# A hybrid attention and convolution block on Trainium2: two more taps of the second convolution block in the second pair, three more in the third, none in the fourth, and the branch's norm started among the fourth pair's projections

## The chip, the core and the metric

The kernel runs on one core of one Trainium2 chip. The metric is the device time of one execution in microseconds (us), lower is better. All times of instructions come from one profiled execution of the kernel before. PE is TensorE's matmul queue, PEld its weight loads, DVE is VectorE, ACT is ScalarE, POOL is GpSimd, SP is SyncE, which issues most of the DMAs.

## The reference

The input is 1024 latent positions and 256 context positions of 1024 channels, all in float32. They are normalised and modulated, and one projection gives eleven column groups to three branches. Their outputs, side by side, go through one output projection, a gated residual and a final norm. The change lies in the third branch (`conformer_branch`) and in the time that the second branch (`neighbourhood_attention`) leaves for it.

```python
def layernorm(x, g, b):
    xf = x.astype(jnp.float32)
    mu = jnp.mean(xf, axis=-1, keepdims=True)
    var = jnp.mean(jnp.square(xf - mu), axis=-1, keepdims=True)
    y = (xf - mu) * lax.rsqrt(var + LN_EPS)
    return (y * g.astype(jnp.float32) + b.astype(jnp.float32)).astype(x.dtype)

def short_conv_branch(z_h, z_b, z_c, z_g, w_conv):
    return z_b * dwconv(z_c * z_h, w_conv) * jax.nn.silu(z_g)

def conformer_branch(z_p, z_q, z_g, w_conv, b_conv, ln_g, ln_b):
    u = z_p * jax.nn.sigmoid(z_q)
    u = dwconv(u, w_conv) + b_conv.astype(u.dtype)
    u = layernorm(u, ln_g, ln_b)
    return jax.nn.silu(u) * jax.nn.silu(z_g)
...
    hl = rmsnorm(x, norm_g[l]) * (1.0 + scale[:, None, :]) + shift[:, None, :]
    hc = rmsnorm(ctx, norm_g[l]) * (1.0 + scale_c) + shift_c
    zl = jnp.split(hl @ w_in[l], PROJ_SPLITS, axis=-1)
...
    ya = short_conv_branch(zl[0], zl[1], zl[2], zl[3], conv_sc[l])
    yb = neighbourhood_attention(heads(zl[4]), heads(zl[5]), heads(zl[6]), kc, vc, rpb[l])
    yb = yb * jax.nn.silu(zl[7])
    yc = conformer_branch(zl[8], zl[9], zl[10], conv_cf[l], conv_cf_b[l], ln_cf_g[l], ln_cf_b[l])
    y = jnp.concatenate([ya, yb, yc], axis=-1) @ w_out[l]
```

The convolution of the third branch has 31 taps over positions, for 256 channels, which are two blocks of 128. Its layer norm runs over the 256 channels of one position, so it needs all taps of both blocks. Attention has 8 heads of 64 channels; each query sees a window of the grid with a bias, and all context keys.

## The kernel before

**Matmuls.** Channels lie on partitions, positions along the free axis. Every matrix product is made of three matmuls on split operands (high weight by high input, high by low, low by high): lines L329, L330 and L331 for one step of 128 input channels by 512 positions. Eight such steps fill one bank (`ps_z`) of which there are three; then a *sink* empties it. The weights of one projection come in two loads (L310, tile `wr`), and each is split: the high part on ACT (L129, `wh`), the low part on POOL (L130, `wl`), or on DVE where the weights of k are scaled on the way (L322).

**The stages.** After the start and the projections of the first two heads come the values of all heads, and then four heads' pairs, one after the other; the code numbers them 0 to 3, and the text says first to fourth. A pair first makes q and k (`proj_pair`): two banks for q (sink L357 on ACT and L358 on DVE), two for k and half a bank for the context keys (sink L379 on ACT and L380 on DVE, each once for each of the pair's two heads). Then `attend` runs 16 blocks of attention, each one head by 128 queries, with 48 steps of projection work (the *fill*: the pair's gate first, then what the other two branches need) strewn between them, so that PE has work while the softmax runs elsewhere. The last pair's fill is its gate, half of the second short convolution's input, and its middle part (`sc_mid`). After the pairs come what is left of the fill, the third branch's gate, and the output projection.

**A block of attention.** Scores go to the one score tile `ps_s` (L596 window keys, L597 context keys). DVE adds the bias and finds the minimum (L601, which has a second row for the readout of `mn`), ACT takes the exponential with its sum (L604), DVE the reciprocal (L605), POOL scales (L606, tile `pr`). Two blocks later PE transposes (L615, `ps_t`), ACT and DVE write the high and low part (L619, L620, `pw`), and one block later PE multiplies by the values (L627, `po`). After two blocks `fold` adds the parts of `po` into `yb` (L572 on ACT, L576 and L578 on DVE). The queries of four blocks are copied by two DMAs (L364) ahead of the blocks that read them.

**The third branch.** Its taps are DVE instructions over 128 channels by 1024 positions, one for each tap (L692 for all but the first of a block), which add into one tile (`acc`). The first block's 31 run while the values are made. The second block's 31 are dealt out to the second, third and fourth pair by `conv_part`: 13, 13 and 5. When all are done `cf_norm` runs in eight steps, two halves of four. A step of the first kind transposes 256 positions to put channels on the free axis (four L713), takes statistics (L718, L719 on DVE), a reciprocal root on POOL (L269, L271), and normalises (two L724 on DVE). Two of these are followed by two steps of the second kind, which transpose back (four L734), apply tanh on ACT (L736) and two DVE passes (L739, L741) into `acc`. Each step uses a bank of `ps_z`, from the same three that the projections use, and each half of the norm uses four of the tiles `t`.

**What sets the order.** On PE the order is that of the code: `run` takes projection steps one after the other, and each PE group adds its estimated length to a clock (`self.pe`). A piece given to `spawn` is put in between: its next part comes when that clock has passed its due time, which is the delay given, and then the gap that the piece yields (1.6 between taps, 3.0 between steps of the norm). On the other engines a list scheduler orders the instructions; each tap is only tied to come after the matmul that stood before it in the code. Every engine runs its own list strictly in order.

Of the kernel before, what the change touches and what calls it, by code (L numbers as in the profile page):

```python
# [65 lines left out]
class Builder:  # L66
# [985 lines left out]
    def build(self):  # L1052
# [68 lines left out]
        for pair in range(1, 4):  # L1121
            self.pair_alloc()
            self.v_alloc()
            self.v_load(pair)
            self.spawn(self.conv_part((13, 13, 5)[pair - 1], 1.6))
            self.run(self.proj_pair(pair))
            if pair == 3:
                self.spawn(self.cf_norm(), 6.0)
            self.attend(pair, itertools.chain(self.proj_gate(pair), fill), MF[pair])
        self.run(fill)  # L1130
        self.drain()
# [83 lines left out]
```

## Time and profile before

| | us |
|---|---|
| median of 3 runs | 612.09 (611.95 to 612.26) |
| the profiled execution | 610.97 |
| its span (first to last instruction) | 609.2 |
| the second pair's q and k, from | 215.3 |
| its attention, from | 242.6 |
| the third pair's q and k, and attention, from | 301, 329.05 |
| the fourth pair's q and k, and attention, from | 386.6, 414.15 |
| what follows the fourth attention, from | 479.5 |

The granted clock of TensorE was 0.997 of full speed over the span. In the rows of a timeline the first number is the start in us from the start of the span, the second the duration in us; then come engine, line, operation, output and input tiles with partitions by elements, and in brackets how long the engine had been idle and what ended that. An "x4" joins four instructions in a row, and the duration is then that of all. "64x256" and the like are partitions by elements of one instruction. The recorded ends of matmuls are modelled, so a group of matmuls is best measured from its start to the next one's.

### The profile page before, as it was taken

How to read it: one execution, taken by the hardware profiler on the slowest of the kernel's cores; microseconds unless marked ns; L12 is line 12 of the kernel's file. 1: busy time of each engine (PE TensorE's matmuls, PEld its weight loads, DVE VectorE, ACT ScalarE, POOL GpSimd, SP SyncE). 2: the span in 40 equal slices, each digit the busy share in tenths (PEclk: the TensorE clock that was granted, in tenths of full speed). 3: DMA queues.
4: the chain of work that ended last, by engine and by line, in shares of the span. 5: the costliest groups of instructions: out<-in, count | busy, mean ns of one | idle time of the engine just before them, and what ended most of it. 6: DMA issues, size and time to landing. Idle time of an engine off the chain costs nothing.

```text
span 609.2 us, 8937 instructions
## 1 busy us (share of the span) xinstructions
PE 589.7 (97%) x3101; PEld 493.8 (81%) x3101; DVE 400.7 (66%) x681; ACT 245.9 (40%) x470; POOL 182.1 (30%) x194
## 2 busy tenths in 40 slices
PE   7899999999999999999999999999999999999995
PEld 5566888888888888888888888888788888888885
DVE  4466988765676699578897666936889447383222
ACT  2555822111455432544423554425645334124222
POOL 1021233000443222333112332113433370099311
PEclk9999999999999999999999999999999999999998
DMA  8992585976533136332145242172301454951122
GB/s 285 356 335 63 190 272 169 115 156 180 121 86 77 24 91 167 75 81 54 41 138 128 48 113 56 45 215 65 81 19 36 137 166 147 341 177 36 70 103 104
DMA packets 97170, 78.64 MB, mean 129 GB/s; under 512 B 26507, under 2 KB 80869, under 8 KB 96997
## 3 DMA queue, kind: packets, MB, share of 16 engines
q1 hardware_dynamic: 95397, 71.51, 42.4%
q10 hardware_dynamic: 1728, 6.55, 3.0%
q8 instruction: 25, 0.41, 0.3%
q14 instruction: 20, 0.16, 0.1%
HBM read 55.93 MB, written 14.29 MB: 115 GB/s over the span
## 4 chain that ended last, share of the span: by engine, by line
PE 84%; DVE 5%; ACT 3%; issue 2%; DMA 2%; POOL 2%; SPq 1%; POOLq 0%; DVEq 0%; ACTq 0%
PE ps_z L329 14%; PE ps_z L331 14%; PE ps_z L330 14%; PE po L627 5%; PE ps_f L878 5%; PE ps_f L879 5%; PE ps_f L877 5%; PE ps_t L615 4%; PE ps_z L419 3%; PE ps_z L421 3%; PE ps_s L596 3%; PE ps_z L420 3%; PE ps_s L597 2%; DMA wr<-in_w_in 2%; PE ps_h L279 1%
## 5 line engine op out<-in xcount | busy, mean ns | idle before, releaser
L329 PE MATMUL ps_z<-h,wh 128*128 128x512 f32 x384 | 151.1, 394 | 0.0
L331 PE MATMUL ps_z<-h,wl 128*128 128x512 f32 x384 | 150.3, 391 | 0.0
L330 PE MATMUL ps_z<-h,wh 128*128 128x512 f32 x384 | 149.8, 390 | 0.0
L130 POOL TENSOR_TENSOR wl<-wr,wh 128x512 fp32r<-128x512 f32 x44 | 60.8, 1384 | 167.3 <-ACT wh L129 160.3
L606 POOL TENSOR_SCALAR pr<-pr,sm 128x640 f32<-128x640 f32 (+1 forms) x64 | 56.6, 884 | 138.2 <-DVE sm L605 118.1
L331 PEld LDWEIGHTS ps_z<-h,wl 128*128 128x128 f32 x384 | 72.1, 188 | 16.1
L330 PEld LDWEIGHTS ps_z<-h,wh 128*128 128x128 f32 x384 | 72.1, 188 | 12.4
L329 PEld LDWEIGHTS ps_z<-h,wh 128*128 128x128 f32 x384 | 72.1, 188 | 12.1
L692 DVE SCALAR_TENSOR_TENSOR acc<-t,half_w,acc 128x1024 f32<-128x1024 f32 x60 | 81.1, 1351 | 1.2
L619 ACT ACTIVATE pw<-ps_t 128x640 fp32r<-128x640 f32 (+1 forms) x64 | 43.5, 680 | 90.1 <-PE ps_t L615 89.9
L601 DVE CUSTOM_DVE_ANT_0 ps_s<-ps_s,bt 128x640 f32<-128x640 f32 (+1 forms) x64 | 50.9, 796 | 29.4 <-PE ps_s L597 27.1
L620 DVE TENSOR_TENSOR pw<-ps_t,pw 128x640 fp32r<-128x640 f32 (+1 forms) x64 | 50.4, 788 | 16.0 <-ACT pw L619 15.8
L604 ACT ACTIVATE pr<-ps_s,mn 128x640 f32<-128x640 f32 (+1 forms) x64 | 49.0, 766 | 19.4 <-DVE mn L601 18.5
L627 PE MATMUL po<-pw,vt 128*128 128x256 f32 x304 | 51.3, 297 | 4.1 <-DVE yb L578 3.1
L878 PE MATMUL ps_f<-wol,y 128*128 128x512 f32 (+1 forms) x136 | 51.6, 379 | 0.0
L879 PE MATMUL ps_f<-woh,y 128*128 128x512 f32 (+1 forms) x136 | 51.5, 379 | 0.0
L877 PE MATMUL ps_f<-woh,y 128*128 128x512 f32 (+1 forms) x136 | 51.5, 379 | 0.0
L129 ACT ACTIVATE wh<-wr 128x512 fp32r<-128x512 f32 x46 | 29.0, 630 | 42.3 <-PE ps_z L330 21.0
L627 PEld LDWEIGHTS po<-pw,vt 128*128 128x128 f32 x304 | 40.5, 189 | 6.4 <-issue 4.7
L615 PE MATMUL ps_t<-ident,pr 128*128 128x128 f32 x304 | 43.6, 272 | 0.0
L596 PE MATMUL ps_s<-kt,qd 128*128 128x384 f32 (+1 forms) x128 | 39.6, 331 | 0.5 <-ACT pr L604 0.4
L615 PEld LDWEIGHTS ps_t<-ident,pr 128*128 128x128 f32 x304 | 35.6, 141 | 1.4 <-issue 0.4
(177 smaller groups left out, 923.9 us busy)
## 6 DMA issues: line engine op xcount, KB each, us to landing
wr<-in_w_in SPq DMA_DIRECT2D x52, 256.0 KB
wa<-in_w_ada SPq DMA_DIRECT2D x16, 512.0 KB
qd<-qn SPq DMA_DIRECT2D x32, 256.0 KB
vd<-t SPq DMA_DIRECT2D x20, 256.0 KB
x_in<-in_x SPq DMA_DIRECT2D x8, 512.0 KB
t<-in_w_ada SPq DMA_DIRECT2D x16, 256.0 KB
vt<-vd SPq DMA_DIRECT2D x32, 128.0 KB
fraw<-in_w_out SPq DMA_DIRECT2D x8, 512.0 KB
```

The lines of the kernel that those rows point to most:

```text
L130: i2 = (eng or nc.vector).tensor_tensor(out=lo, in0=src, in1=f32(hi), op=ALU.subtract)
L329: nc.tensor.matmul(ps, lhsT=wh, rhs=hh, start=(k == 0), stop=False)
L330: nc.tensor.matmul(ps, lhsT=wh, rhs=hl, start=False, stop=False)
L331: self.last = nc.tensor.matmul(ps, lhsT=wl, rhs=hh, start=False, stop=(k == KT - 1))
L596: nc.tensor.matmul(win, lhsT=q[:, b % 4], rhs=kwin, start=(i == 0), stop=(i == 1))
L606: nc.gpsimd.tensor_scalar(out=pr, in0=pr, scalar1=sm, scalar2=0.5, op0=ALU.mult, op1=ALU.mult)
L615: nc.tensor.transpose(out=pt[:, c * P:(c + 1) * P], in_=pr[:, c * P:(c + 1) * P], identity=self.ident)
L627: self.nc.tensor.matmul(po, lhsT=vt[:, vi, h], rhs=pw[:, c], start=(c == 0), stop=(c == n - 1))
L692: self.after_pe(nc.vector.scalar_tensor_tensor(out=acc, in0=u[:, t:t + T], scalar=self.half_w[:, 2 * t + ct:2 * t + ct + 1], in1=acc, op0= ...
L877: nc.tensor.matmul(ps, lhsT=yh, rhs=wh[:, ch], start=(first and i == 0), stop=False)
L878: nc.tensor.matmul(ps, lhsT=yh, rhs=wl[:, ch], start=False, stop=False)
L879: nc.tensor.matmul(ps, lhsT=yl, rhs=wh[:, ch], start=False, stop=(last and i == len(chs) - 1))
```

## The change

The taps of the second block are dealt out 15, 16 and 0 in place of 13, 13 and 5, and `cf_norm` is spawned ahead of the fourth pair's q and k with a delay of 2.0, in place of after them with 6.0. Its eight steps are unchanged, and so is their gap.

```diff
             self.v_load(pair)
-            self.spawn(self.conv_part((13, 13, 5)[pair - 1], 1.6))
+            self.spawn(self.conv_part((15, 16, 0)[pair - 1], 1.6))
+            if pair == 3:
+                self.spawn(self.cf_norm(), 2.0)
             self.run(self.proj_pair(pair))
-            if pair == 3:
-                self.spawn(self.cf_norm(), 6.0)
             self.attend(pair, itertools.chain(self.proj_gate(pair), fill), MF[pair])
```

How this moves instructions is seen best at three places. The first is DVE in the second pair, from the last two sinks of k to the first block's softmax; `64x8x8x8` is a sink of 512 latent keys, `64x256` one of the context keys. Before:

```order
L692 SCALAR_TENSOR_TENSOR acc<-t_1472,half_w,acc 128x1024
L380 TENSOR_TENSOR kt<-ps_z,kt 64x8x8x8
L380 TENSOR_TENSOR kt<-ps_z,kt 64x256 x2
L601 ISA ps_s,mn<-ps_s,bt_1194 128x512
L601 ISA mn 128x1
L605 RECIPROCAL sm<-sm 128x1
```

And in the changed kernel, at the same place:

```order
L692 SCALAR_TENSOR_TENSOR acc<-t_1472,half_w,acc 128x1024
L380 TENSOR_TENSOR kt<-ps_z,kt 64x8x8x8
L692 SCALAR_TENSOR_TENSOR acc<-t_1472,half_w,acc 128x1024
L380 TENSOR_TENSOR kt<-ps_z,kt 64x256
L692 SCALAR_TENSOR_TENSOR acc<-t_1472,half_w,acc 128x1024
L380 TENSOR_TENSOR kt<-ps_z,kt 64x256
L601 ISA ps_s,mn<-ps_s,bt_1194 128x512
L601 ISA mn 128x1
L605 RECIPROCAL sm<-sm 128x1
```

The two added taps stand ahead of the sinks of the context keys, and so ahead of the first block's L601. The third pair has the same rows, and its third added tap stands behind the first L601 and ahead of the L605.

The second place is DVE at the start of the fourth pair, where the third pair's last blocks end (L620, and the fold, L576 and L578) and the sinks of q begin (L358). Before:

```order
L576 TENSOR_TENSOR yb<-po,fold 64x16x16
L578 TENSOR_TENSOR yb<-po,yb 64x16x16
L692 SCALAR_TENSOR_TENSOR acc<-t_1472,half_w,acc 128x1024 x2
L620 TENSOR_TENSOR pw<-ps_t,pw 128x4x128
L692 SCALAR_TENSOR_TENSOR acc<-t_1472,half_w,acc 128x1024
L358 TENSOR_TENSOR qn<-ps_z,qn 128x8x8x8
```

And in the changed kernel, where `t_4018` and `t_4061` are the normalised tiles of the first two steps:

```order
L576 TENSOR_TENSOR yb<-po,fold 64x16x16
L718 BN_STATS bnst<-ps_z 128x6
L578 TENSOR_TENSOR yb<-po,yb 64x16x16
L719 BN_AGGR bnmv<-bnst 128x2
L718 BN_STATS bnst<-ps_z 128x6
L719 BN_AGGR bnmv<-bnst 128x2
L724 TENSOR_SCALAR t_4018<-ps_z,bnmv,bnrs 128x256 x2
L620 TENSOR_TENSOR pw<-ps_t,pw 128x4x128
L718 BN_STATS bnst<-ps_z 128x6 x2
L719 BN_AGGR bnmv<-bnst 128x2 x2
L724 TENSOR_SCALAR t_4061<-ps_z,bnmv,bnrs 128x256 x2
L358 TENSOR_TENSOR qn<-ps_z,qn 128x8x8x8
```

Taps are gone from this place, and the first two steps of the norm stand around the L620 of the third pair's last block and ahead of the first sink of q. The second half of the norm stands among the sinks of k in the same way.

The third place is SP's list of DMAs at the start of the fourth pair, as one piece of the difference.

```order
 L444 DMA vt<-vd 128x2x256
 L563 DMA yd_63<-yb 128x1024
+L310 DMA wr<-in_w_in 128x4x128 x2
 L364 DMA qd<-qn 64x2x512 x4
-L310 DMA wr<-in_w_in 128x4x128 x4
+L310 DMA wr<-in_w_in 128x4x128 x2
 L509 DMA bt_1198<-u_1053 24x1x64
```

Two of the four weight loads (L310) that stood behind the q loads (L364) stand ahead of them.

## The prediction

> **What bounds the kernel now.** I read the page first: the busy shares, then the chain that ended last. TensorE (PE) is busy for 97% of the span and carries 84% of the chain, so a microsecond counts only where PE stands still for it.
>
> ```profile
> PE 589.7 (97%) x3101; PEld 493.8 (81%) x3101; DVE 400.7 (66%) x681; ACT 245.9 (40%) x470; POOL 182.1 (30%) x194
> PE 84%; DVE 5%; ACT 3%; issue 2%; DMA 2%; POOL 2%; SPq 1%; POOLq 0%; DVEq 0%; ACTq 0%
> ```
>
> Then the table of stretches, for the stages that the change touches: the attention of the second pair, the projections of the fourth, the attention of the fourth, where the norm now runs. The columns are the stretch, its length, and busy us and instructions of PE, weight load, DVE, ACT and POOL.
>
> ```profile
> 240.50:301.00 60.50, 60.30 (x356) 52.95 (x355) 43.23 (x94) 31.58 (x66) 20.83 (x22) 1.00 0.25 61
> 386.60:414.10 27.50, 27.50 (x141) 23.41 (x140) 14.95 (x20) 8.48 (x16) 6.14 (x5) 1.00 0.48 135
> 414.10:480.00 65.90, 62.78 (x381) 54.02 (x381) 52.32 (x124) 33.81 (x67) 22.90 (x30) 1.00 0.20 47
> ```
>
> PE idles 60.50 - 60.30 = 0.2 us in the second pair's attention, nothing in the fourth pair's projections, and 65.90 - 62.78 = 3.1 us in the fourth pair's attention. The second pair fills its attention with the same work as the fourth (a gate, half of a short-convolution input, its middle), but has no norm. So moving the norm aims at about 2.9 us of idle PE, and those projections have DVE time to spare (14.95 of 27.50 us).
>
> **The norm leaves the fourth pair's attention.** What it costs there is idle time (two rows of the table of waits of 414 to 480: sum, count, longest) and starts that come late (the timeline):
>
> ```profile
> PE po L627 <- DVE yb L578: 1.6, 2, 0.9
> PE ps_z L734 <- DVE t L724: 0.9, 2, 0.5
> ...
> 429.91 0.78 PE L734 MATMUL ps_z<-ident,t 128*128 128x128 f32 x2 [0.38 <-DVE t L724]
> 430.46 0.41 PE L596 MATMUL ps_s<-kt,qd 128*128 128x384 f32 x1
> 434.77 0.60 PE L734 MATMUL ps_z<-ident,t 128*128 128x128 f32 x4
> 435.13 0.42 PE L596 MATMUL ps_s<-kt,qd 128*128 128x384 f32 x1
> 463.90 0.83 PE L627 MATMUL po<-pw,vt 128*128 128x256 f32 x5 [0.76 <-DVE yb L578]
> ```
>
> The idle part is 3.1 - 0.2 = 2.9 us. Some waiting is counted as busy: two transposes took 0.55 us to the next start at 429.91, where four that waited for nothing took 0.36 us at 434.77, so some 0.37 us is hidden. I estimate 1.9 us at six such places. Together 4.8 us. The wait of 0.76 us at 463.90 lies behind the short convolution's taps, after the norm's end; I leave it, so **-4.1 us**. Bounds: the norm's own two waits (0.9) and the longer fold wait (0.9) alone, -1.8; everything, -4.8. The 32 transposes themselves, eight groups of about 0.36 us, move and are paid in either place.
>
> **The norm arrives among the projections.** There are now eight more tenants for the three z banks, and the order on DVE puts each norm step in line with the sinks of q and k. One step takes, by its rows here:
>
> ```profile
> 441.72 0.60 PE L713 MATMUL ps_z<-ident,acc 128*128 128x128 f32 x4
> 442.36 0.76 DVE L718 BATCH_NORM_STATS2 bnst<-ps_z 128x6 f32<-128x256 f32 x2 [0.85 <-PE ps_z L713]
> 443.70 0.70 POOL L271 TENSOR_TENSOR bnrs<-bnrs,mhalf 128x2 f32<-128x2 f32 x1
> 444.44 1.00 DVE L724 TENSOR_SCALAR t<-ps_z,bnmv,bnrs 128x256 f32<-128x256 f32 x2 [0.15 <-POOL bnrs L271]
> ...
> 393.10 0.63 PE L627 MATMUL po<-pw,vt 128*128 128x256 f32 x4
> 393.57 0.39 PE L329 MATMUL ps_z<-h,wh 128*128 128x512 f32 x1
> 394.26 0.40 PE L329 MATMUL ps_z<-h,wh 128*128 128x512 f32 x1
> ...
> 410.74 0.63 ACT L129 ACTIVATE wh<-wr 128x512 fp32r<-128x512 f32 x1 [0.70 <-PE ps_z L330]
> 435.46 0.78 ACT L736 ACTIVATE t<-ps_z,half_ln 128x512 f32<-128x512 f32 x1 [0.76 <-PE ps_z L734]
> ```
>
> From the transposes' start to the normalised tile is 445.44 - 441.72 = 3.7 us. Between a second group of L713 and the L734 that reads it, PE has some 3.3 us (four steps of 394.26 - 393.57 = 0.69, a values group of 393.57 - 393.10 = 0.47) in the first half, 3.4 us (five steps) in the second. In the first half, DVE comes to the statistics 0.4 us late, behind L620: PE waits about 0.4 + 3.7 + 0.05 - 0.4 (the transposes' own time) - 3.25, which is 0.5 us. In the second half two L380 sinks of 0.69 us stand in between, of which about 0.7 us is not covered: again 0.5. A third wait follows at the gate: its bank is that of k's second half, and the second L379 of that sink now stands behind a weight split (L129, 0.63 us) that itself waits for PE, 0.4 us. Sum **+1.4 us**. Bounds: 0 if PE's lead holds everywhere, and 2.7 if one split on POOL (L130, 1.29 us) also gets ahead of a reciprocal root. Behind a waiting L724 stand the L620 of the third pair's last block and the L358 of q; PE needs neither before its next wait. On SP two weight loads now precede the four q loads; these are issued some 4 us later, and still land well before the scores. ACT's four tanh of 0.78 us have ACT's 19 idle us. The five taps that leave these projections delayed no PE instruction (its idle there is 0), so they give nothing.
>
> **Two taps more in the second pair, three in the third.** DVE does not run them in a gap: the order puts tap 14 ahead of the first L380 of the context keys, and tap 15 ahead of the second, which stands ahead of the first block's bias pass, L601. The rows at that place, second pair:
>
> ```profile
> 239.36 1.29 DVE L692 SCALAR_TENSOR_TENSOR acc<-t,half_w,acc 128x1024 f32<-128x1024 f32 x1
> 240.02 3.04 POOL L130 TENSOR_TENSOR wl<-wr,wh 128x512 fp32r<-128x512 f32 x2 [11.12 <-ACT wh L129]
> 240.68 0.69 DVE L380 TENSOR_TENSOR kt<-ps_z,kt 64x512 fp32r<-64x512 f32 x1
> 241.66 0.42 DVE L380 TENSOR_TENSOR kt<-ps_z,kt 64x256 fp32r<-64x256 f32 x1 [0.30 <-ACT kt L379]
> 242.53 0.43 DVE L380 TENSOR_TENSOR kt<-ps_z,kt 64x256 fp32r<-64x256 f32 x1 [0.45 <-ACT kt L379]
> 242.71 0.28 PE L597 MATMUL ps_s<-kt,qd 128*128 128x256 f32 x1
> 243.26 0.70 DVE L601 CUSTOM_DVE_ANT_0 ps_s<-ps_s,bt 128x512 f32<-128x512 f32 x1 [0.31 <-PE ps_s L597]
> 244.11 0.69 ACT L604 ACTIVATE pr<-ps_s,mn 128x512 f32<-128x512 f32 x1 [1.62 <-DVE mn L601]
> 244.70 0.19 ACT L604 ACTIVATION_READ_ACCUMULATOR pr<-ps_s,mn 128x1 f32 x1
> 245.15 0.34 PE L596 MATMUL ps_s<-kt,qd 128*128 128x384 f32 x1
> ```
>
> There is one score tile (ps_s): the second block's scores at 245.15 need the first block's exponential, which ends at 244.70 + 0.19 = 244.89. With the 0.05 to 0.15 us of a hand-over the slack is 0.1 us. So what L601 loses beyond 0.1 us PE loses, and nothing later gives it back: PE's own work between scores is fixed, and the next block's chain is as tight.
>
> How late is L601? Unhindered: tap 14 from 241.40, L380 at 242.71, tap 15 at 243.15, L380 at 244.46, L601 at 244.92: 1.66 us late, 1.55 us lost. But POOL splits weights at that moment, and taps and splits do not run at once:
>
> ```profile
> 224.77 1.29 POOL L130 TENSOR_TENSOR wl<-wr,wh 128x512 fp32r<-128x512 f32 x1 [9.25 <-ACT wh L129]
> 224.85 2.29 DVE L692 SCALAR_TENSOR_TENSOR acc<-t,half_w,acc 128x1024 f32<-128x1024 f32 x1
> ```
>
> A tap issued 0.08 us behind a split took 2.29 us in place of 1.28. At 240.02 it was the other way round: the first split sat through tap 13 (to 240.65), and the pair ended at 243.06, 1.2 us each. So tap 14 meets the first split: it starts at 241.7 and ends at 242.95; the second split takes 242.95 to 244.1, L380 runs beside it, tap 15 starts at 243.9 and ends at 245.2, the last L380 ends at 245.65, and L601 starts at 245.7: 2.44 late, **2.3 us lost**. If both splits run ahead of tap 14, it is 246.4 and 3.0 us. The third pair's rows repeat this place to within 0.1 us, its splits included; its third tap (16) stands behind L601, where ACT's 0.9 us of exponential hide most of it, and if that cover is gone a reciprocal comes 0.4 us later into 2.6 us of slack before the transposes that need it. So twice 2.3, **+4.6 us**; bounds 3.1 and 6.0.
>
> [...]
>
> **Sum.** -4.1 + 1.4 + 4.6 = +1.9 us. The profiled execution took 610.97 us (span 609.2), so 612.9 by its own clock. The median of the runs, 612.09, is 1.1 us above it; added there, **614.0 us**.
>
> **Rivals.**
> 1. *No collision.* DVE gets in before each split, taps cost 1.55 each: +3.1 + 1.4 - 4.1 = +0.4, 612.5 us. For it: at 240.02 POOL waited. Against: tap 14 comes due while the first split runs.
> 2. *Faster: the score chain absorbs the taps.* If PE waits only for the first context keys (L597 at 243.2 in place of 242.7, 0.5 us), and the second block's scores do not follow L601, then 1.0 + 1.4 - 4.1 = -1.7, 610.4 us. It decides at the second L596 of each attention: it needs 1.5 us of slack there. Against it stand 244.89 and 245.15.
> 3. *Much slower.* Splits run ahead of both taps (6.0), and a root waits for a split on POOL (2.7), against the same gain: +4.6, 616.7 us.
> 4. *The change doesn't do what it says.* The order shows both moves, so this is left only as part of the cases above: the fold waits may stay without the norm (gain 1.8), for +4.2, 616.3 us.
>
> **How the numbers follow.** The forecast has 0.48 (its own range 613 to 615.5), rival 1 0.22, rival 2 0.13, rivals 3 and 4 together 0.17. A measurement of this kernel tells about 0.2%, 1.2 us, from no change. Faster by more: rival 2, 0.13. Within: rival 1 and a tenth of the forecast, 0.27. Slower: the rest, 0.60. The range runs from rival 2 to a little beyond rival 3: 610.2 to 617.0.
>
> **What would show it.** Right: PE waits of 0.5 to 1 us before the first L597 of the second and third attention and over 1 us before the second L596; taps of over 2 us beside L130 there; idle PE under 1.2 us in the fourth attention; waits for L724 in the fourth projections, 1.4 us with the gate's. Wrong: second scores on time in spite of late L601, or a fourth attention that keeps its 3 us of idle PE.

## The result, and the profile after

The changed kernel takes 615.58 us (median of 4 runs, 615.51 to 616.27), the kernel before 612.06 (4 runs, 611.95 to 612.26). The ratio is 1.006, with a 95% interval of 1.0042 to 1.0077: slower by 3.5 us, where 1.9 was forecast. The time lies just above the forecast's own range, 613 to 615.5 us, and within the range over all cases, 610.2 to 617.0.

The profiled execution took 615.57 us (span 613.8), which is 4.6 us more than that of before. Not all of this belongs to the change. The table gives the start of a block's first scores in the two timelines.

| scores of | before | after | later by |
|---|---|---|---|
| first attention, first block | 156.82 | 157.52 | 0.7 |
| second attention, first block | 242.59 | 243.28 | 0.7 |
| second attention, third block | 247.86 | 250.78 | 2.9 |
| third attention, first block | 329.04 | 331.96 | 2.9 |
| third attention, third block | 334.31 | 339.46 | 5.15 |
| third attention, last block | 381.78 | 386.96 | 5.2 |
| fourth attention, first block | 414.15 | 424.85 | 10.7 |
| fourth attention, last block | 469.74 | 474.46 | 4.7 |

The 0.7 us arise before the first scores, where both programs are alike. In the fourteen profiles of this study these scores start between 156.8 and 158.5 us, and the profile of before is among the earliest. What is left are three steps: 2.23 us at the start of the second attention, 2.23 at that of the third, and in the fourth pair 5.52 more among the projections and 5.98 less in the attention, so 0.46 us gained.

First the table of stretches of the changed kernel: the second attention, the fourth pair's projections, the fourth attention, each between the same instructions as before. Columns: stretch, length, busy us of PE, weight load, DVE, ACT and POOL with their counts, then granted clock.

```profile
241.20:303.93 62.73, 60.82 (x356) 52.86 (x355) 46.45 (x96) 31.65 (x66) 21.78 (x22) 1.00 0.24 59
391.78:424.80 33.02, 32.11 (x173) 26.53 (x172) 24.10 (x47) 11.25 (x20) 8.72 (x12) 1.00 0.43 118
424.80:484.70 59.90, 58.26 (x350) 50.59 (x350) 42.32 (x93) 30.45 (x63) 19.10 (x21) 1.00 0.21 49
```

PE now idles 1.9 us in the second attention (0.2 before), 0.9 us in the projections (nothing before), and 1.6 us in the fourth attention (3.1 before). The idle time moved more than it went.

The timeline at the start of the second attention shows the taps:

```profile
240.79 3.92 POOL L130 TENSOR_TENSOR wl<-wr,wh 128x512 fp32r<-128x512 f32 x2 [11.20 <-ACT wh L129]
241.37 0.69 DVE L380 TENSOR_TENSOR kt<-ps_z,kt 64x512 fp32r<-64x512 f32 x1
242.09 1.49 DVE L692 SCALAR_TENSOR_TENSOR acc<-t,half_w,acc 128x1024 f32<-128x1024 f32 x1
...
243.61 0.42 DVE L380 TENSOR_TENSOR kt<-ps_z,kt 64x256 fp32r<-64x256 f32 x1
244.06 1.73 DVE L692 SCALAR_TENSOR_TENSOR acc<-t,half_w,acc 128x1024 f32<-128x1024 f32 x1
...
244.09 0.39 PE L597 MATMUL ps_s<-kt,qd 128*128 128x256 f32 x1 [0.53 <-DVE kt L380]
...
245.83 0.43 DVE L380 TENSOR_TENSOR kt<-ps_z,kt 64x256 fp32r<-64x256 f32 x1
246.28 0.70 DVE L601 CUSTOM_DVE_ANT_0 ps_s<-ps_s,bt 128x512 f32<-128x512 f32 x1
...
247.72 0.19 ACT L604 ACTIVATION_READ_ACCUMULATOR pr<-ps_s,mn 128x1 f32 x1
247.97 0.44 PE L596 MATMUL ps_s<-kt,qd 128*128 128x384 f32 x1 [1.18 <-ACT pr L604]
```

On the clock of before (0.69 earlier) L601 starts at 245.59 in place of 243.26, and the second block's scores at 247.28 in place of 245.15. PE waits 0.53 us for the context keys and 1.18 us for the exponential. The third attention shows the same rows, and its tap behind L601 costs nothing.

In the fourth pair, these are all waits of PE that the table of waits lists, first of the projections, then of the attention (sum, count, longest):

```profile
PE ps_z L734 <- DVE t L724: 0.5, 1, 0.5
PE ps_z L329 <- DVE kt L380: 0.2, 1, 0.2
...
PE po L627 <- DVE yb L578: 1.0, 1, 1.0
PE ps_s L596 <- ACT pr L604: 0.6, 1, 0.6
```

And the timeline of PE there, with the starts to be read against each other (the rows at 422.26 and 422.73 are the end of k and the start of the gate, and the last pair belongs to the attention):

```profile
396.73 0.60 PE L713 MATMUL ps_z<-ident,acc 128*128 128x128 f32 x4
397.09 0.48 PE L329 MATMUL ps_z<-h,wh 128*128 128x512 f32 x1
397.40 0.39 PE L330 MATMUL ps_z<-h,wh 128*128 128x512 f32 x1
...
400.18 0.40 PE L331 MATMUL ps_z<-h,wl 128*128 128x512 f32 x1
401.10 0.63 PE L734 MATMUL ps_z<-ident,t 128*128 128x128 f32 x4 [0.53 <-DVE t L724]
...
416.66 1.22 PE L734 MATMUL ps_z<-ident,t 128*128 128x128 f32 x4
417.64 0.48 PE L329 MATMUL ps_z<-h,wh 128*128 128x512 f32 x1
...
422.26 0.28 PE L331 MATMUL ps_z<-hc,wl 128*128 128x256 f32 x1
422.73 0.47 PE L329 MATMUL ps_z<-h,wh 128*128 128x512 f32 x1 [0.19 <-DVE kt L380]
...
429.17 0.40 PE L331 MATMUL ps_z<-h,wl 128*128 128x512 f32 x1
430.13 0.44 PE L596 MATMUL ps_s<-kt,qd 128*128 128x384 f32 x1 [0.56 <-ACT pr L604]
```

A matmul of 512 columns takes 0.23 us from start to start (399.95 to 400.18). So the wait at 401.10 is 401.10 - 400.18 - 0.23 = 0.69 us. The group at 416.66 takes 0.98 us where one that waits for nothing takes 0.36 (396.73 to 397.09): 0.62 us of waiting, all counted as busy. Each group of transposes costs 0.36 us and another 0.08 in the L329 behind it (397.40 - 397.09 = 0.31 in place of 0.23), so 0.44. Eight of them are 3.5 us, the two waits 1.3, and the gate's wait for its bank 0.35 (422.73 - 422.26, less 0.12 for 256 columns, the mean of the two steps from 422.02 to 422.26), which leaves 0.3 of the 5.52 us in small pieces. A group cost the same 0.44 us in the attention before: behind the one at 441.72 the L329 starts at 442.08 and its L330 at 442.39.

The last pair of rows is the wait for the third block's scores. Before, the norm's first transposes lay in it:

```profile
418.70 0.60 PE L713 MATMUL ps_z<-ident,acc 128*128 128x128 f32 x4
419.42 0.44 PE L596 MATMUL ps_s<-kt,qd 128*128 128x384 f32 x1
```

From the second block's scores to the third's it was 419.42 - 416.70 = 2.72 us before, and it is 430.13 - 427.39 = 2.74 now. Nothing was gained there by taking four transposes away.

### The profile page after: what moved, and what is told of

Its sections match the earlier page's. It is cut to its first block, busy times and chain, and to the rows that moved or that the text cites. A ratio compares the mean times of both kernels' runs of the same rounds, so it can differ in the third digit from the quotient of the medians.

```text
span 613.8 us, 8942 instructions
## 1 busy us (share of the span) xinstructions
PE 590.5 (96%) x3101; PEld 493.0 (80%) x3101; DVE 406.5 (66%) x681; ACT 245.3 (40%) x470; POOL 183.6 (30%) x194
## 5 line engine op out<-in xcount | busy, mean ns | idle before, releaser
L329 PE MATMUL ps_z<-h,wh 128*128 128x512 f32 x384 | 151.6, 395 | 0.2 <-DVE kt L380 0.2
L330 PE MATMUL ps_z<-h,wh 128*128 128x512 f32 x384 | 149.8, 390 | 0.0
L130 POOL TENSOR_TENSOR wl<-wr,wh 128x512 fp32r<-128x512 f32 x44 | 62.5, 1423 | 148.9 <-ACT wh L129 142.7
L606 POOL TENSOR_SCALAR pr<-pr,sm 128x640 f32<-128x640 f32 (+1 forms) x64 | 55.2, 863 | 147.0 <-DVE sm L605 129.5
L692 DVE SCALAR_TENSOR_TENSOR acc<-t,half_w,acc 128x1024 f32<-128x1024 f32 x60 | 82.4, 1373 | 1.3
L329 PEld LDWEIGHTS ps_z<-h,wh 128*128 128x128 f32 x384 | 72.2, 188 | 12.4 <-PE ps_z L331 0.4
L330 PEld LDWEIGHTS ps_z<-h,wh 128*128 128x128 f32 x384 | 72.2, 188 | 12.4
L601 DVE CUSTOM_DVE_ANT_0 ps_s<-ps_s,bt 128x640 f32<-128x640 f32 (+1 forms) x64 | 51.0, 797 | 31.2 <-PE ps_s L597 28.2
L620 DVE TENSOR_TENSOR pw<-ps_t,pw 128x640 fp32r<-128x640 f32 (+1 forms) x64 | 50.5, 789 | 19.0 <-ACT pw L619 18.9
L604 ACT ACTIVATE pr<-ps_s,mn 128x640 f32<-128x640 f32 (+1 forms) x64 | 49.0, 766 | 21.7 <-DVE mn L601 21.2
L627 PE MATMUL po<-pw,vt 128*128 128x256 f32 x304 | 51.3, 297 | 3.3 <-DVE yb L578 2.4
L627 PEld LDWEIGHTS po<-pw,vt 128*128 128x128 f32 x304 | 40.5, 189 | 5.5 <-issue 2.6
```

The costliest lines, as they stand in the source:

```text
L130: i2 = (eng or nc.vector).tensor_tensor(out=lo, in0=src, in1=f32(hi), op=ALU.subtract)
L329: nc.tensor.matmul(ps, lhsT=wh, rhs=hh, start=(k == 0), stop=False)
L330: nc.tensor.matmul(ps, lhsT=wh, rhs=hl, start=False, stop=False)
L601: nc.vector.tensor_tensor_reduce(s, s, tb, op0=ALU.add, op1=ALU.min, scale=1.0, scalar=3e38, accum_out=mn)
L606: nc.gpsimd.tensor_scalar(out=pr, in0=pr, scalar1=sm, scalar2=0.5, op0=ALU.mult, op1=ALU.mult)
L627: self.nc.tensor.matmul(po, lhsT=vt[:, vi, h], rhs=pw[:, c], start=(c == 0), stop=(c == n - 1))
```

## The experiments

The runs came in four sets, and each set was timed against the kernel before on the same chip. Its medians there were 611.88 (the first four rows below), 611.94 (the next four), 612.00 (three) and 611.87 us (the last).

| run | us | ratio, 95% interval |
|---|---|---|
| taps only | 615.98 | 1.0071, 1.0059 to 1.0084 |
| one more tap | 613.79 | 1.0035, 1.0022 to 1.0047 |
| late taps | 614.17 | 1.0041, 1.0028 to 1.0055 |
| late taps, norm moved | 613.48 | 1.0027, 1.0017 to 1.0036 |
| taps behind the bias pass | 611.79 | 1.0000, 0.9991 to 1.0009 |
| the same, norm spread | 610.51 | 0.9979, 0.9971 to 0.9988 |
| taps denser | 618.48 | 1.0108, 1.0094 to 1.0123 |
| no split | 614.40 | 1.0048, 1.0035 to 1.0060 |
| norm earlier | 610.68 | 0.9980, 0.9970 to 0.9989 |
| first step alone | 614.00 | 1.0035, 1.0023 to 1.0046 |
| norm moved as in the change, taps behind the bias pass | 611.13 | 0.9988, 0.9979 to 0.9997 |
| last step in a wait | 609.13 | 0.9961, 0.9948 to 0.9975 |

### The two parts apart, and the dose

Taps only, and one more tap (with `(14, 14, 3)`); the norm as before in both:

```diff
-            self.spawn(self.conv_part((13, 13, 5)[pair - 1], 1.6))
+            self.spawn(self.conv_part((15, 16, 0)[pair - 1], 1.6))
```

> The taps are dealt out 15, 16 and 0 as in the change, the norm stays in the fourth pair's attention. Theory (the parts add; the traces of before and after show 2.2 us lost at the second scores of the second and third attention, and 0.5 us gained by the norm's move): +4.5 on 612.06, so 616.5 us (616.1 to 617.0), with the second scores of both attentions 2.1 us later against the first ones than before. Rival (the taps' loss is what pushes the norm's gain away, since both shift the same chains): no more than 615.6 us.

> The taps are dealt out 14, 14 and 3, the norm stays: one tap more than before ahead of the context keys' sinks in the second and third pair. Theory (a tap ahead of the first sink of the context keys makes L601 late by its own length, less what overlaps with ACT's sink): L601 1.0 to 1.2 us late, 0.9 to 1.1 us lost in each pair, so 613.9 to 614.3 us. Rival (VectorE has 1.2 us idle in these projections, 25.5 of 26.7 busy, and a tap of 1.3 us fits into it): within 0.3 us of before, 612.4 us.

Taps only: +4.1 us by the medians, 0.1 us short of the theory's range and 0.4 above the rival's (the traces have 4.45), and the second scores come 2.11 us later against the first ones in both attentions, the third another 0.1. So the taps' loss is the same with the norm in either place. One more tap: +1.9 us, again 0.1 us short of the theory's range and far from the rival's; in the trace 0.86 us in the second pair and 0.88 in the third. One tap doesn't fit into DVE's 1.2 idle us, since 0.75 us of these lie between the sinks, where DVE waits for ACT (before, 0.30 us ahead of 241.66 and 0.45 ahead of 242.53).

### Is it the split on POOL?

The two splits at the start of the second and third attention become a memset, taps as in the change, norm as before:

```diff
+        if not low:
+            self.nc.scalar.activation(out=wh, in_=wr, func=AF.Copy)
+            self.nc.gpsimd.memset(f32(wl), 0.0)
```

> Taps 15, 16 and 0, the norm stays; the low part of the weights that POOL splits at 240 us and 327 us (short convolution, first block: c in the second pair's attention, gate in the third's) is a memset of zero on POOL in place of the subtraction, so these products lack their low part. Theory (taps and splits exclude each other: taps 14 and 15 took 1.49 and 1.73 us beside the splits, 0.64 us more than two free ones): both taps take 1.29 us, L601 is 0.6 us less late, 1.6 us lost in each pair in place of 2.2, so 1.2 us less than with taps alone on the same chip: 614.7 us, 614.3 to 615.1. Rival (the lateness is the taps' own length, the split costs nothing): 615.9 us.

614.40 us, within the theory's range. The timeline, in which three added lines of code make L692 L695, L380 L383 and L601 L604:

```profile
240.84 0.52 POOL L320 MEMSET wl<- 128x512 f32 x1 [0.89 <-PE ps_z L334]
...
241.50 1.28 DVE L695 SCALAR_TENSOR_TENSOR acc<-t,half_w,acc 128x1024 f32<-128x1024 f32 x1
...
243.26 1.28 DVE L695 SCALAR_TENSOR_TENSOR acc<-t,half_w,acc 128x1024 f32<-128x1024 f32 x1
...
245.04 0.70 DVE L604 CUSTOM_DVE_ANT_0 ps_s<-ps_s,bt 128x512 f32<-128x512 f32 x1
```

Both taps take 1.28 us, and the loss is 1.58 us in each pair (from the starts of the scores) in place of 2.23. So 0.65 us of each loss come from the splits and 1.58 from the taps' own length: what the prediction's first rival gave as 1.55. Neither of these two taps meets a POOL instruction any more (the memset ends at 241.36). Tap 13 does: it starts at 239.46 beside the other memset (239.43, 0.53 us) and takes 1.28 us as well. So this memset did not hold a tap up, where beside the splits the two added taps took 1.49 and 1.73 us; what in the split does was not shown.

### Place or number?

Five taps leave the projections and go between blocks: two in the second and three in the third attention. "Late taps" has 7.3 and 12.0 in the added line (gap and delay), "taps behind the bias pass" 3.3 and 2.2; the second run has the norm moved as well.

```diff
-            self.spawn(self.conv_part((13, 13, 5)[pair - 1], 1.6))
+            self.spawn(self.conv_part((13, 13, 0)[pair - 1], 1.6))
             self.run(self.proj_pair(pair))
+            self.spawn(self.conv_part((2, 3, 0)[pair - 1], 3.3), 2.2)
```

> The taps are dealt out 13, 13 and 0 among the projections, and the five that are left are put between blocks of the second attention (two) and the third (three), 7.3 us apart, behind the fifth block's start; the norm stays. Theory (the loss hangs on the place, the first block's L601, not on the number of taps: later blocks are 3.6 us apart and their L601 has over 1 us to spare): 612.1 us, 611.8 to 612.6. Rival (VectorE is the limit of an attention, and each tap costs about its own 1.3 us wherever it stands): 5 times 0.9 to 1.3 more, 616.5 to 618.5 us.

> As the run before with late taps (13, 13, 0 among the projections, two and three between later blocks), and the norm among the fourth pair's projections as in the change. Theory (the norm's move gains 0.5 us net, by the traces): 611.6 us, 611.2 to 612.0. Rival (the move gains the 2.7 us of the prediction, and the taps' loss hid it): 609.4 us.

> 13, 13 and 0 taps among the projections; the two and three that are left now stand right behind the readout of L601 of the first and second block of the second and third attention, ahead of L605, and the third one behind the fourth block's L605, ahead of the next L601. The norm stays. Theory (a tap is free where ACT's exponential covers it, or where L601 has slack; the second late taps of the run before cost 0.9 and the third 0.5 because they stood ahead of a fold and of an L620): 611.9 us, 611.5 to 612.5. Rival (each tap in an attention beyond the first costs 0.5 to 0.9 us): 613.5 to 614.5 us.

Late taps: 614.17 us, between theory and rival. In its trace the first late tap of each attention costs nothing, the second 0.9 us, the third 0.5. The second one in the second attention:

```profile
266.09 1.27 DVE L692 SCALAR_TENSOR_TENSOR acc<-t,half_w,acc 128x1024 f32<-128x1024 f32 x1
...
267.28 0.41 DVE L576 TENSOR_TENSOR yb<-po,fold 64x256 f32<-64x256 f32 x1
...
268.22 0.41 DVE L578 TENSOR_TENSOR yb<-po,yb 64x256 f32<-64x256 f32 x1
...
268.78 0.83 PE L627 MATMUL po<-pw,vt 128*128 128x256 f32 x5 [0.68 <-DVE yb L578]
```

It stands ahead of a fold, and the next values wait for the one `po` tile that the fold frees. Taps behind the bias pass: 611.79 us, as before to within 0.6 us either way, with all five taps in the attentions. The first one in the second attention:

```profile
244.01 0.70 DVE L601 CUSTOM_DVE_ANT_0 ps_s<-ps_s,bt 128x512 f32<-128x512 f32 x1 [0.22 <-PE ps_s L597]
244.63 1.28 DVE L692 SCALAR_TENSOR_TENSOR acc<-t,half_w,acc 128x1024 f32<-128x1024 f32 x1
245.83 0.15 DVE L605 RECIPROCAL sm<-sm 128x1 f32<-128x1 f32 x1
...
245.89 0.34 PE L596 MATMUL ps_s<-kt,qd 128*128 128x384 f32 x1
```

The second scores are 245.89 - 243.34 = 2.55 us behind the first ones, as before. So the place decides, not the number, and taking five taps out of the fourth pair's projections gives nothing, as predicted.

The norm's move gains 614.17 - 613.48 = 0.7 us on late taps; the run itself missed its 611.6, which had counted on taps that cost nothing. Where they cost nothing, it was run again:

> As the run with taps behind the bias pass, and the norm moved exactly as in the change (2.0, all gaps 3.0): the change's second part without any loss from the taps. Theory (5.5 us more among the projections, 6.0 less in the attention): 611.3 us, 611.0 to 611.7. Rival (the 2.7 us of the prediction): 609.1 us.

611.13 us, 0.7 less than 611.79; the trace has +5.53 among the projections and -5.9 in the attention. So the move gains 0.5 to 0.7 us by the traces and the medians, not 2.7; each ratio is known to 0.6 us either way, so the smallness of the gain rests on the traces as well.

### Would an earlier start do?

```diff
+            self.spawn(self.conv_part((15, 16, 0)[pair - 1], 1.3))
```

> Taps 15, 16 and 0 as in the change, 1.3 in place of 1.6 apart, the norm stays. They then stand ahead of the last sinks of the latent keys and none between the two sinks of the context keys. Theory (VectorE is busy 25.5 of the 26.7 us of these projections and 2.6 us more do not fit, whatever the spacing; what comes back is the time in which VectorE waited for ACT between those sinks, about 0.9 us in each pair): 614.2 us, 613.8 to 615.6. Rival (the spacing is the cause, and started earlier the taps fit): 612.1 to 612.8 us.

618.48 us: both failed. Now the taps stand ahead of the latent keys' sinks, whose two halves on ACT and DVE take turns (in the changed kernel such a sink's L380 at 421.89 waited 0.90 us for its L379); in the second pair two of them, from 240.22, took 3.60 us beside a split at 241.46, where two free ones took 2.60 (234.83). The trace is of the slowest of five executions, 622.07 us. The two rows are PE's longest waits, in the second and third attention. Behind them are rows of the table of stretches, with the granted clock behind POOL's count:

```profile
246.73 0.39 PE L597 MATMUL ps_s<-kt,qd 128*128 128x256 f32 x1 [1.75 <-DVE kt L380]
...
337.56 0.58 PE L597 MATMUL ps_s<-kt,qd 128*128 128x256 f32 x1 [2.10 <-DVE kt L380]
```

```profile
246.70:252.00 5.30, 5.27 (x19) 4.54 (x20) 1.84 (x5) 1.16 (x3) 1.16 (x2) 0.68 0.24 63
...
337.50:343.00 5.50, 5.44 (x15) 4.57 (x16) 1.35 (x5) 1.16 (x3) 0.97 (x2) 0.50 0.23 61
```

PE waited 1.75 and 2.10 us, and in the 5.3 and 5.5 us from the end of the wait its granted clock was 0.68 and 0.50. This is not so in every execution: in two of the five, of 617.04 and 618.16 us, the clock over the whole span was 0.999, and they too lie above both expectations. In the changed kernel, where PE waits 0.53 and 1.18 us at this place, that clock stayed at 1.00:

```profile
247.90:252.00 4.10, 4.03 (x22) 3.42 (x23) 1.97 (x6) 1.39 (x4) 1.50 (x2) 1.00 0.06 15
```

### The norm's own waits

Norm spread: as taps behind the bias pass, the norm started ahead of the fourth projections with a delay of 0.6, and two gaps changed:

```diff
                 vts.append(vt)
                 self.pe(0.43)
-                yield 3.0
+                yield (3.0, 3.7)[g]
...
                 self.pe(0.43)
-                yield 3.0
+                yield 2.6
```

> The taps as in the run with taps behind the bias pass; the norm among the fourth pair's projections, started at 0.6 in place of 2.0, with a gap of 3.7 in place of 3.0 between the second normalised tile and its backward transposes, and 2.6 after those. Theory (of the 5.5 us that the projections grew, 1.3 us are the two waits for L724, which the longer gap takes away; the move without them gains 0.5 + 1.3): 610.1 us, 609.6 to 610.7. Rival (the wait only goes on to the next bank, since the norm holds one of three banks for longer than PE needs for a half projection's step): 0.5 us gained, 611.4 us.

610.51 us: nearly the whole of it. The projections grew by 3.89 us in place of 5.53, the two waits for L724 are gone. But 0.84 us came up at the second scores:

```profile
420.69 0.69 DVE L741 SCALAR_TENSOR_TENSOR acc<-t,acc 128x512 f32<-128x512 f32 x1
421.41 0.70 DVE L601 CUSTOM_DVE_ANT_0 ps_s<-ps_s,bt 128x512 f32<-128x512 f32 x1
...
423.10 0.45 PE L596 MATMUL ps_s<-kt,qd 128*128 128x384 f32 x1 [0.69 <-ACT pr L604]
```

The norm's last L741 now stands directly ahead of the first L601 and makes it late, as the changed kernel's tap 15 did from one sink further ahead. Two ways to move it:

> As the run that spread the norm, with the norm started at 0.3, and gaps of 2.7, 3.7 and 2.0 in place of 3.0, 3.7 and 2.6: its last L734 stands eight steps ahead of the first scores, and its last L741 ahead of the sinks of the context keys. Theory (the 0.84 us that were lost at the second scores of the fourth attention came from an L741 that stood between the last context sink and L601): 609.7 us, 609.2 to 610.3, second scores 2.6 us behind the first ones. Rival (steps that follow each other faster make PE wait for a bank instead): 610.5 us or more.

610.68 us, no better and in the rival's range: 0.60 of the 0.84 us stayed, and the projections grew by 4.19 us in place of 3.89. L741 now stood ahead of the context keys' sinks, took 1.59 us beside a split on POOL in place of 0.69, and made L597 wait. Of what the rival named there is little: a wait of PE of less than 0.2 us ahead of the gate.

> As the run with taps behind the bias pass, and of the norm only the first step (four L713 and what follows them) taken out of the fourth attention and put among the projections, twelve steps ahead of the first scores; the other seven stand where they stood. Theory (in the attention these transposes lay in a wait of PE that belongs to the score chain and stays without them; among projections they cost 0.4 us): 612.2 us, 0.4 more than 611.8, the third block's scores 2.7 us behind the second's as before. Rival (what the prediction counted: the transposes cost 0.36 us in either place and the late start beside them goes): 611.4 us, and the third block's scores 0.7 us earlier against the second's.

This run tried the wait at 419.42 by itself. In the stretch in question the theory holds: PE waits 0.59 us there without the transposes, and the third scores are 2.72 us behind the second, as before; the projections grew by 0.54. The whole is 614.00 us though, 1.8 more than expected, since the scheduler now put L724 ahead of the fifth block's L601:

```profile
431.07 1.22 PE L734 MATMUL ps_z<-ident,t 128*128 128x128 f32 x4
431.82 0.83 DVE L601 CUSTOM_DVE_ANT_0 ps_s<-ps_s,bt 128x640 f32<-128x640 f32 x1
...
433.73 0.44 PE L596 MATMUL ps_s<-kt,qd 128*128 128x384 f32 x1 [1.45 <-ACT pr L604]
```

DVE stood 2.44 us for the reciprocal root with the bias pass behind it, PE waited 0.6 and 1.45 us, and for the next 3.3 us its clock was 0.55. (The trace is of the slowest of seven executions, 612.93 to 615.34 us.) So the total says nothing on the first step; the stretch does. The last run used it the other way round, and put the norm's last step into that wait:

```diff
-                yield 3.0
+                yield (2.6 if half == 0 or ct else 8.5)
```

> As the run that spread the norm, but its last step (four L734, L739, L741) comes two steps behind the second block's scores of the fourth attention, in the wait that PE has there before the third block's scores, with a gap of 8.5 in place of 2.6 ahead of it. Theory (no L741 stands ahead of the first L601, which gives back 0.84 us, and the transposes lie in a wait that stays anyway, another 0.4 us among the projections): 609.3 us, 608.9 to 609.9; the second and the third scores 2.6 and 2.7 us behind those before them. Rival (L739 and L741 now stand ahead of the third block's L605 and make its chain late instead): 610.3 us or more.

```profile
422.88 0.60 PE L734 MATMUL ps_z<-ident,t 128*128 128x128 f32 x4
423.63 0.44 PE L596 MATMUL ps_s<-kt,qd 128*128 128x384 f32 x1
```

609.13 us, 0.9961 of before (0.9948 to 0.9975). The third scores are 423.63 - 420.92 = 2.71 us behind the second ones, the four transposes cost nothing there, and the projections, with seven groups left, grew by 3.45 us in place of 3.89. This version beats both kernels, and it has both of the change's ideas, with the five taps and the norm's last step in places where the traces had shown time to spare.

## Why the prediction was right, and where it was not

**The taps: +4.6 forecast, 4.45 in the traces.** The chain was the one that the prediction set out: taps and splits at odds, both sinks and L601 late, one score tile, no slack. It had L601 at 245.7 and it came at 245.59. Taking the splits away left 1.58 us a pair, and moving the taps behind L601 left nothing, so these two links were tried by themselves; that there is only one score tile was read from the rows and not tried. The first rival, no collision, is out by the 0.65 us of the splits, and the second, 1.5 us of slack in the score chain, because PE waited 1.18 us at just that place. One sign failed: the taps took 1.49 and 1.73 us beside L130 and not over 2, though the prediction's own rows, with tap 14 from 241.4 to 242.95, already had 1.55.

**The norm: -2.7 forecast, -0.5 in the trace.** That the norm makes PE start late in the attention and wait among the projections came true; both sizes were off. Eight groups of transposes, 3.5 us with what they add to the instruction behind them, moved from one stage to the other. Beside them the attention gave -5.98 + 3.5 = -2.5 where -4.1 was forecast, and the projections took 5.52 - 3.5 = +2.0 where +1.4 was.

The step that failed is "Some waiting is counted as busy", where all six late starts were put down to the norm. That at 418.70 was the score chain's own wait: the 0.37 us stayed, and the 0.36 us of its transposes, which had been free there, were now paid elsewhere, 0.7 us in all. The fold's wait at 463.90, which the prediction left where it was, grew by 0.3 us (0.76 before, 1.04 after). Another 0.2 us came up in the changed kernel ahead of the L627 at 447.70. And the late starts were put at 4.8 us, or 4.1 without that fold; read from start to start before, the six places give 0.37, 0.95, 0.26, 1.02, 1.10 and, at the fold, 0.92 us, so 3.7 without it and 0.4 less than forecast. Together that is the 1.6 us that are missing. So the sign "idle PE under 1.2 us in the fourth attention" failed: it is 1.6 us.

Among the projections the two waits for L724 were sized at 0.5 each and took 0.69 and 0.62. For the second the prediction's own terms, 3.7 + 0.05 - 0.4 + 0.7 - 3.4, give 0.65 and not 0.5. The third wait, at the gate, was 0.35 in place of 0.4, and it ended with the sink of k as described. The 0.3 us that are left stay unexplained.

**The sum.** +1.9 forecast, +3.5 by the medians. Of the 4.6 us between the two profiled executions 0.7 lie ahead of any changed instruction. The prediction had noticed that its profile was 1.1 us below the median and added them; the traces show the start as one place where executions differ. The direction came out because the taps, sized to within 0.2 us, outweigh the norm, whose gain was five times too large. The result lies nearer to rival 4 (616.3) than to the forecast (614.0), but for the most part not by its story: of the two fold waits only the one at 463.90 stayed.

## What to carry to other kernels

A stage with idle time on an engine is not a stage with room: of DVE's 1.2 us 0.75 lay between sinks that wait for another engine, and what counted was which instruction stood ahead of the one that frees the only score tile. Place fill work behind that instruction and not ahead of it; the same five taps cost 4 us or nothing. Before counting a wait as a gain, ask what would end next at that place, since work that lies in another chain's wait is free where it is and costs its full length where it goes.

## What was not expected of the hardware

A pause of PE can cost twice. With denser taps, after waits of 1.75 and 2.10 us, the granted clock was 0.68 and 0.50 over the next 5.3 and 5.5 us, and with the first step alone, after waits of 0.6 and 1.45 us in one stretch of 2.7 us, it was 0.55 over 3.3 us; in the changed kernel waits of 0.53 and 1.18 us, within 4.4 us, left it at 1.00.

The clock's record in the traces shows when it changed. With denser taps the clock stood at 0.50 from 248.15 to 251.56 and from 336.90 to 343.72, once 3.41 us and once 6.82. In the run with the first step alone it stood there from 434.06 to 437.47, 3.41 us. That the waits brought the falls is the author's reading of where these lie; what makes the clock fall, and why some executions of one kernel lose it and others don't, was not shown: no trace shows an execution of these two kernels without a fall.
